# Low parts of weight tiles by accumulating DMAs in place of subtractions

## The chip, the cores and the metric

The kernel runs on one core of a Trainium2 chip. The metric is the device time of one execution in microseconds; the median of three is given. In the profile's names PE is TensorE (matrix products), PEld its weight loads, DVE is VectorE, ACT is ScalarE, POOL is GpSimd and SP is SyncE, which issues most loads.

## The reference

Two layers of an encoder on 512 tokens of 1024 features, in float32:

```python
def rms_norm(x, g):
    y = xf * lax.rsqrt(jnp.mean(xf * xf, axis=-1, keepdims=True) + RMS_EPS)
    return (y * g.astype(F32)).astype(x.dtype)

def swiglu_ffn(x, w_gate, w_up, w_down):          # 1024 -> 2816 -> 1024
    return (jax.nn.silu(x @ w_gate) * (x @ w_up)) @ w_down

for layer in range(DEPTH):                        # DEPTH = 2
    f = swiglu_ffn(rms_norm(h, g[0]), ffn_w_gate[layer, 0], ffn_w_up[layer, 0], ffn_w_down[layer, 0])
    h = h + 0.5 * rms_norm(f, g[1])
    hn = rms_norm(h, g[2])
    # layer 0: m = concat(pool_mixer(z[:512]), s5_mixer(z[512:])) @ ab_w_out, z = hn @ ab_w_in
    # layer 1: m = neighborhood_attention(hn, na_w_qkv, na_rpb, na_w_out)
    h = h + rms_norm(m, g[3])
    f = swiglu_ffn(rms_norm(h, g[4]), ffn_w_gate[layer, 1], ffn_w_up[layer, 1], ffn_w_down[layer, 1])
    h = h + 0.5 * rms_norm(f, g[5])
```

## The kernel before

**Products.** Each float32 operand is split into two 12-bit parts, hi + lo. A product is three passes over parts (`mm3`, L170 to L172): hi x hi, then one low part with the other's hi, then the reverse. In the projections of features on partitions the third pass, L172, takes the weights' low part.

**Weight tiles.** The class `Weights` makes all 128 x 1024 tiles in the order of their use. `_load` has SP load a raw tile from DRAM (`w_raw`, two buffers). `hi` copies it on ScalarE into `w_hi`, which rounds it (L113). `lo` subtracts: `w_lo` = raw - hi (L124), on VectorE, or on GpSimd where a call says so. `fill(n)` emits these splits until n tiles beyond those used up are split; it follows each tile's products (`done`, n = 4), so splits run three to four tiles ahead. `w_hi` and `w_lo` have five buffers.

**Plain tiles and pairs.** In each of the four feed-forwards a part of the gate and up tiles is "plain" (kind p: 24 matmuls of 512 columns). The others are taken as pairs of tiles in Winograd's form: seven products of 12 matmuls of 256 columns, on four derived tiles called g, s, u, h. Tile g is the raw tile itself; s, u and h are sums: `sums` makes them with L95 and L96 on VectorE and L98 on GpSimd. After each pair VectorE adds up the results (L594, L600, L602, and L574 last, when the pair's last product has ended). A gate pair then goes through ScalarE's Silu (L578), the up pair behind it through GpSimd's product with it (L576). `sums` of a pair and its g are emitted after the g product of the pair before it.

**Stages.** Feed-forward (up products, then the down products in two halves), mixer (layer 0: pooling and state space; layer 1: attention), feed-forward, for each layer. Between stages there is a transition: `finish_rows` ends the down products by pairs of token tiles, while the norm of the next stage (`pre_norm`, `to_xT`) runs on ScalarE and VectorE, and `fill(2)`, `fill(4)` split the first tiles of the next stage there, on GpSimd. In the first feed-forward the tables of the state-space mixer are made beside the products by VectorE, ScalarE and DMAs that GpSimd issues. Each engine works through its instructions in the order in which the program emits them.

Of the kernel before, what the change touches and what calls it, by code (L numbers as in the profile page):

```python
# [37 lines left out]
class Weights:  # L38
    """Weight tiles [128, 1024] in the order of their use: loaded, then split into two
    12-bit parts (hi + lo is the float32 value exactly), both ahead of the products.  # L40
    A pair of tiles G = [A11 A12], U = [A21 A22] that is multiplied by Winograd's form of
    Strassen's scheme becomes the tiles g = [A11 A12], s = [S3 -S2], u = [S1 A22], h = [S4]
    with S1 = A21 + A22, S2 = S1 - A11, S3 = A11 - A21, S4 = A12 - S2."""
# [3 lines left out]
    def __init__(self, nc, pool, items, n_split=5):  # L47
# [3 lines left out]
        for item in items:  # L51
            z = {}
# [7 lines left out]
        self.lo_engine = nc.vector  # L60

    def _load(self, tag=None):
# [12 lines left out]
        z[kind] = t  # L75
        self.loaded += 1
# [23 lines left out]
    def source(self, kind, z):  # L100
        """What a tile is split from."""
        if kind in "pg":
            return self._raw("raw", z)
        return {"s": lambda: z["s"], "u": lambda: z["u"][:, HALF:], "h": lambda: z["u"][:, :HALF]}[kind]()

    def hi(self):
        kind, z = self.tiles[self.n_hi]
        src = self.source(kind, z)
        n = src.shape[-1]
        hi, lo = (self.pool.tile([P, 1024], F32R, tag=t, bufs=self.n_split, name=t) for t in ("w_hi", "w_lo"))  # L110
        step = n if kind == "p" else HALF
        for k in range(0, n, step):
            self.nc.scalar.copy(hi[:, k:k + step], src[:, k:k + step])  # L113
        self.hi_lo[self.n_hi] = (hi, lo)
        self.n_hi += 1

    def lo(self, engine=None):
# [6 lines left out]
        (engine or self.lo_engine).tensor_tensor(out=lo[:, :n], in0=src, in1=hi[:, :n].bitcast(F32), op=ALU.subtract)  # L124
# [6 lines left out]
    def fill(self, n, lo_engine=None):  # L131
        """Emits splits until n tiles are split and not used up, loads further."""
# [23 lines left out]
    def done(self, n=1, fill=True):  # L156
        """The products of n more tiles are emitted."""
# [5 lines left out]
class Builder:  # L163
# [14 lines left out]
    def new_psum(self, *halves, **tags):  # L178
        """All eight banks anew: of one kind, or some for each of the tags (number, or number
        and columns), or half for each of two groups of names."""  # L180
# [11 lines left out]
    def rsqrt(self, v):  # L192
        """1 / sqrt(v) of a column pair."""
# [3 lines left out]
    def rsqrt_steps(self, v):  # L197
        """1 / sqrt(v), by steps that return what becomes of it: exponent-halving guess y
        within 3.5%, then y * (1 + d)^(-1/2) for d = v y^2 - 1, by its minimax polynomial on
        that range."""  # L200
# [27 lines left out]
    def chain_begin(self, pool, scale):  # L228
        """What follows a projection m: h += scale * rms_norm(m) * gain, by pairs of token tiles."""
# [5 lines left out]
    def post_pair(self, pair, half, ps):  # L235
        """The vector engine reads one bank while the scalar engine reads the other."""
# [18 lines left out]
    def residual(self, ts, parts=1):  # L255
        """By parts of the columns, each yielded when it is done."""
# [19 lines left out]
    def pre_norm(self, pool, pair, s, gain, order):  # L276
        """Rows of a token pair over their rms; what is returned transposes and splits them."""
# [12 lines left out]
    def to_xT(self, xn, pair, gain, order, between, by_tile=False):  # L290
        """by_tile: the transposes of the first row tile go ahead of all others."""
# [33 lines left out]
    def part(self, x, order, pair):  # L325
        """The columns of a [128, 512] operand that hold the tokens of a pair of token tiles."""
# [10 lines left out]
    def proj_steps(self, ps, w, order, pair=None):  # L337
        """ps[128 output features, tokens] = W[:, 128 columns]^T xT, a step per two k-tiles."""
# [12 lines left out]
    def first_proj(self, n, order, before, start=None, each=None, after=None):  # L351
        """The first n column tiles on the first token pair (the first two by turns), while the
        second pair's norm ends.
        start: what follows that; each: what follows a tile, after: what stands for the
        splits that follow it."""
# [24 lines left out]
    def split_evac(self, hi, lo, src, scale=None, later=None):  # L380
        """hi on the scalar engine, lo on the vector engine; that can be left for later, so
        that the vector engine does not wait for the scalar engine."""
# [18 lines left out]
    def finish_rows(self, cp, psB, tail, kts, lhs, opened, nxt):  # L401
        """The last k-tiles of the second half of the columns, by pairs of token tiles, so that
        the norms of one pair run beside the products of the next."""
# [33 lines left out]
        self.W.fill(2, nc.gpsimd)  # L437
# [4 lines left out]
        self.W.fill(4, nc.gpsimd)  # L442
        return self.pre_norm(cp, 1, finish((2, 3)), nxt[0], nxt[1])

# [1 line left out]
    b_order = list(range(NF))  # L446

    def form_product(self, ps, w, x):
        """ps [128, 256] (+)= a quarter: weights [128, 4 x 128]^T times activations [128, 4, 256]."""
# [7 lines left out]
    def x_sums(self, forms, tmp):  # L457
        """The sums of quarters of xT (B) that Winograd's scheme takes, split, and beside them
        the first tiles of weights, by steps that follow the first column tiles:
        T1 = B12 - B11, T3 = B22 - B12, -T2 = T1 - B22, -T4 = B21 - T2."""  # L460
# [48 lines left out]
    def ffn(self, layer, which, nxt, before, ssm=None):  # L509
        """gate/up with features on partitions, down with tokens on partitions. From feature  # L510
        tile n_plain on, gate and up are taken by pairs of tiles (A1, A2), by halves of the
        contraction and of the tokens, in seven products of a quarter (Winograd).
        nxt: (gain row, order) of the norm that follows, None at the end. ssm: the constants of
        the state-space mixer are made beside it."""
# [5 lines left out]
        def start():  # L520
            """Sums of the activations, beside the last four plain tiles."""
# [94 lines left out]
        # ten slots; the first two lie where memory is free first  # L616
# [74 lines left out]
    # tokens by (column, row): a tile of 128 queries is 16 columns, its keys are 24 or 32 columns  # L691
    KEY0 = (0, 64, 192, 320)
    NKEY = (192, 256, 256, 192)
    # chunks of the keys of a query tile: (offset, number, set of V rows, its first partition)
# [3 lines left out]
    def attention(self, nxt, before):  # L698
# [19 lines left out]
        def evac_q(hp, ps):  # L718
            """By heads: both parts as one contraction, the high one in the rows of the head."""
# [8 lines left out]
        def evac_k(hp, ps):  # L728
            """By heads: the high part twice; the low part of both."""
# [28 lines left out]
        def keys(x, s):  # L758
            """Rows of V: set 0 is the last and the first 64 keys, the others 128 from 64 on."""
# [3 lines left out]
        def v_steps(c):  # L763
            """V of four heads, for all sets: weight tiles of four k-tiles by 256 columns."""
# [20 lines left out]
        self.W.lo_engine = nc.gpsimd  # L785
# [110 lines left out]
        self.W.lo_engine = V  # L896
# [22 lines left out]
    # Chunks of 8 tokens: token 8c + j. Lanes are (a, p) for the group 2 gp + a and the state p;  # L919
    # columns are (direction, gp). U[(h', j)] holds the token j of every chunk.  # L920
    #   m_dram  U -> chunk input of the states, [(h', j), unit, re/im, dir, gp, a, p]
    #   g_dram  C lambda^k, k = 1..8 (8..1 for the backward direction), [(re/-im, p), unit, dir, gp, a, (h, k)]
    #   i_dram  U -> outputs of the same chunk, [(h', j'), g, (j, h)]
# [839 lines left out]
```

## Time and profile before

| | |
|---|---|
| median of three runs | 1957.59 us (1957.04 to 1961.34) |
| span of the profiled execution, first to last instruction (its own time) | 1956.6 us |
| busy, share of the span: PE / PEld / DVE / ACT / POOL | 95% / 84% / 78% / 47% / 22% |
| mean granted TensorE clock | 0.983 |
| DMA moved | 225.47 MB, mean 115 GB/s |
| HBM read / written | 206.69 MB / 18.84 MB |

The span is the profiled execution's time; it lies within 1 us of the median. Busy shares are means over stages with different limits. The clock is a share of full speed: 1 is 2.4 GHz, and the lower level, 0.5, is 1.2 GHz.

### The profile page before, as it was taken

The numbers are of one execution on the slowest core, as the hardware profiler recorded it, in microseconds if no ns is written. First come the engines' busy times: TensorE is split into PE (matmuls) and PEld (weight loads), VectorE is DVE, ScalarE is ACT, GpSimd is POOL, SyncE is SP. The second block draws the span as 40 slices with busy tenths as digits, with TensorE's granted clock in tenths as the row PEclk, the third lists the DMA queues.
The fourth block names the chain that finished last, engine by engine and source line by source line (L and its number), as shares of the span: only waits on it lengthen the run. The fifth ranks groups of instructions, "written<-read, shape, count | busy, mean of one in ns | idle before, by whom it ended". The sixth has DMA issues, their size and how long they took to land.

```text
span 1956.6 us, 31540 instructions
## 1 busy us (share of the span) xinstructions
PE 1864.5 (95%) x12368; PEld 1652.2 (84%) x12368; DVE 1519.5 (78%) x2357; ACT 916.9 (47%) x1725; POOL 423.9 (22%) x267
## 2 busy tenths in 40 slices
PE   7999999998889999999899999999999989999998
PEld 7877987886678999888799997879878788999886
DVE  6788979968679999844899996465565589999744
ACT  5244455455454444533544445346555455444432
POOL 1024221014014223100432330011222023322100
PEclk9999999999999999999999999999999999999999
DMA  5464246537422233322223323223222222332321
GB/s 189 136 204 158 104 142 199 186 114 254 150 87 98 101 105 109 108 97 75 76 97 109 108 87 119 97 76 108 98 97 98 73 79 92 103 108 98 119 90 62
DMA packets 82020, 225.47 MB, mean 115 GB/s; under 512 B 15792, under 2 KB 20048, under 8 KB 80848
## 3 DMA queue, kind: packets, MB, share of 16 engines
q1 hardware_dynamic: 70176, 197.80, 29.3%
q0 software_dynamic: 6960, 23.57, 4.0%
q10 hardware_dynamic: 4736, 2.10, 0.4%
q8 instruction: 97, 1.59, 0.3%
q14 instruction: 51, 0.42, 0.1%
HBM read 206.69 MB, written 18.84 MB: 115 GB/s over the span
## 4 chain that ended last, share of the span: by engine, by line
PE 43%; DVE 16%; issue 9%; ACT 5%; DMA 1%; POOL 0%; DVEq 0%; ACTq 0%; POOLq 0%
PE ps_gu L172 4%; PE ps_gu L170 4%; PE ps_gu L171 4%; PE ps_A L172 3%; PE ps_A L170 3%; PE ps_A L171 3%; PE ps_B L172 3%; PE ps_B L171 3%; PE ps_B L170 3%; PE ps_f L170 3%; DVE w_s L96 3%; DVE w_lo L124 2%; PE ps_f L172 2%; PE ps_f L171 2%; ACT w_hi L113 1%
## 5 line engine op out<-in xcount | busy, mean ns | idle before, releaser
L124 DVE TENSOR_TENSOR w_lo<-w_raw,w_hi 128x1024 fp32r<-128x1024 f32 x209 | 275.8, 1325 | 218.4 <-ACT w_hi L113 218.4
L113 ACT CAST w_hi<-w_raw 128x1024 fp32r<-128x1024 f32 (+1 forms) x313 | 261.7, 863 | 270.9 <-PE ps_A L172 83.5
L172 PE MATMUL ps_gu<-xsum,w_lo 128*128 128x256 f32 x1088 | 309.5, 284 | 9.7 <-DVE w_lo L124 9.7
L172 PE MATMUL ps_gu<-xT_hi,w_lo 128*128 128x256 f32 (+1 forms) x1008 | 311.7, 309 | 1.3 <-DVE w_lo L124 1.0
L171 PE MATMUL ps_gu<-xsum,w_hi 128*128 128x256 f32 x1088 | 306.8, 282 | 3.4 <-DVE xsum L470 3.2
L170 PE MATMUL ps_gu<-xsum,w_hi 128*128 128x256 f32 x1088 | 308.0, 283 | 0.0
L170 PE MATMUL ps_gu<-xT_hi,w_hi 128*128 128x256 f32 (+1 forms) x1008 | 307.8, 305 | 0.0
L171 PE MATMUL ps_gu<-xT_lo,w_hi 128*128 128x256 f32 (+1 forms) x1008 | 306.8, 304 | 0.0
L172 PEld LDWEIGHTS ps_gu<-xsum,w_lo 128*128 128x128 f32 x1088 | 207.4, 191 | 11.4 <-DVE w_lo L124 11.4
L171 PEld LDWEIGHTS ps_gu<-xsum,w_hi 128*128 128x128 f32 x1088 | 208.0, 191 | 4.9 <-DVE xsum L470 4.9
L124 POOL TENSOR_TENSOR w_lo<-w_raw,w_hi 128x1024 fp32r<-128x1024 f32 x36 | 86.0, 2393 | 582.0 <-DVE rs_q L215 377.3
L170 PEld LDWEIGHTS ps_gu<-xsum,w_hi 128*128 128x128 f32 x1088 | 208.1, 191 | 0.0
L172 PEld LDWEIGHTS ps_gu<-xT_hi,w_lo 128*128 128x128 f32 x1008 | 191.9, 190 | 17.0 <-DVE w_lo L124 7.6
L170 PEld LDWEIGHTS ps_gu<-xT_hi,w_hi 128*128 128x128 f32 x1008 | 191.9, 190 | 10.0 <-issue 1.1
L171 PEld LDWEIGHTS ps_gu<-xT_lo,w_hi 128*128 128x128 f32 x1008 | 192.2, 191 | 8.7
L98 POOL TENSOR_TENSOR w_u<-w_raw,w_s 128x512 f32<-128x512 f32 x68 | 121.2, 1782 | 277.5 <-ACT w_hi L113 168.1
L113 ACT CAST w_hi<-w_s 128x512 fp32r<-128x512 f32 x136 | 77.5, 619 | 200.0 <-DVE w_s L96 193.5
L172 PE MATMUL ps_A<-w_hi,gT 128*128 128x512 f32 x352 | 141.2, 401 | 12.2 <-DVE gT L630 12.2
L576 POOL TENSOR_TENSOR g<-g,m 128x1024 f32<-128x1024 f32 x34 | 93.0, 2734 | 258.4 <-DVE m L574 258.4
L96 DVE TENSOR_TENSOR w_s<-w_raw,w_u 128x1024 f32<-128x1024 f32 x68 | 145.8, 2143 | 2.4
L170 PE MATMUL ps_A<-w_hi,gT 128*128 128x512 f32 x352 | 140.9, 400 | 0.0
L171 PE MATMUL ps_A<-w_lo,gT 128*128 128x512 f32 x352 | 140.3, 398 | 0.0
(375 smaller groups left out, 4376.7 us busy)
## 6 DMA issues: line engine op xcount, KB each, us to landing
w_raw<-in_w_gu_dram SPq DMA_DIRECT2D x106, 512.0 KB, 3.3
w_raw<-in_w_dn_dram SPq DMA_DIRECT2D x88, 512.0 KB, 3.2
w_u<-in_w_gu_dram SPq DMA_DIRECT2D x70, 512.0 KB, 3.6
w_raw<-in_w_qk_dram SPq DMA_DIRECT2D x16, 512.0 KB, 3.2
bias<-in_att_bias_dram SPq DMA_DIRECT2D x16, 512.0 KB, 4.1
w_raw<-in_w_in_dram SPq DMA_DIRECT2D x8, 512.0 KB, 3.2
cm<-m_dram SPq DMA_DIRECT2D x4, 1024.0 KB, 8.7
w_raw<-in_w_ao_dram SPq DMA_DIRECT2D x8, 512.0 KB, 4.0
```

The costliest lines, as they stand in the source:

```text
L96: tt(out=blocks(s), in0=g[:, :HALF].unsqueeze(1).broadcast_to([P, 2, HALF]), in1=blocks(u)[:, :2], op=ALU.subtract)
L98: self.nc.gpsimd.tensor_tensor(out=u[:, :HALF], in0=g[:, HALF:], in1=s[:, HALF:], op=ALU.add)
L113: self.nc.scalar.copy(hi[:, k:k + step], src[:, k:k + step])
L124: (engine or self.lo_engine).tensor_tensor(out=lo[:, :n], in0=src, in1=hi[:, :n].bitcast(F32), op=ALU.subtract)
L170: mm(ps, a[0], b[0], start=start, stop=False)
L171: mm(ps, a[0], b[1], start=False, stop=False)
L172: mm(ps, a[1], b[0], start=False, stop=stop)
L576: nc.gpsimd.tensor_tensor(out=rows(f), in0=rows(f), in1=m, op=ALU.mult)
```

## The change

The low part of a tile that comes straight from DRAM (kinds p and g) is no longer subtracted by an engine. ScalarE writes the negative of the rounded tile into `w_lo` right behind the copy into `w_hi`, and GpSimd issues a DMA that reads the tile from DRAM once more and adds it onto `w_lo`. The low parts of s, u and h are subtracted by VectorE as before (one of them by GpSimd at each start of the pairs). The choices of GpSimd as the engine for `lo` elsewhere fall away.

```diff
 def _load(self, tag=None):
...
         z[kind] = t
+        z[kind + "_src"] = src
         self.loaded += 1
...
 def hi(self):
...
         for k in range(0, n, step):
             self.nc.scalar.copy(hi[:, k:k + step], src[:, k:k + step])
+        if kind in "pg":
+            self.nc.scalar.mul(lo, src, -1.0)
         self.hi_lo[self.n_hi] = (hi, lo)
...
 def lo(self, engine=None):
...
         if kind == "g":
             self.sums(z)
         hi, lo = self.hi_lo[self.split]
-        (engine or self.lo_engine).tensor_tensor(out=lo[:, :n], in0=src, in1=hi[:, :n].bitcast(F32), op=ALU.subtract)
+        if kind in "pg":
+            self.nc.gpsimd.dma_start(lo, z["raw_src"], accum_op=ALU.add)
+        else:
+            (engine or self.nc.vector).tensor_tensor(out=lo[:, :n], in0=src, in1=hi[:, :n].bitcast(F32),
+                                                     op=ALU.subtract)
...
 def finish_rows(self, cp, psB, tail, kts, lhs, opened, nxt):
...
-        self.W.fill(2, nc.gpsimd)
+        self.W.fill(2)
...
-        self.W.fill(4, nc.gpsimd)
+        self.W.fill(4)
...
 def attention(self, nxt, before):
...
-        self.W.lo_engine = nc.gpsimd
...
-        self.W.lo_engine = V
...
 def first_norm(self, gain, order):
...
-        self.W.lo(nc.gpsimd)
+        self.W.lo()
...
-        self.W.fill(4, nc.gpsimd)
+        self.W.fill(4)
```

Line numbers of the changed kernel differ: L95, L96, L98 are L98, L99, L101 there, L124 is L132, L574 and L576 are L583 and L585, L594, L600 and L602 are L603, L609 and L611; the negative is L118 and the accumulating DMA L130.

GpSimd's queue at the start of the second feed-forward's pairs and for the pairs next behind it (L485 and L486 make a sum of the activations `xT_hi` and `xT_lo`; the name `g` is the buffer that these and the feed-forward's product L576 are kept in); before:

```order
L98 TENSOR_TENSOR w_u<-w_raw,w_s 128x512
L485 TENSOR_TENSOR g<-g,xT_hi 128x1024
L486 TENSOR_TENSOR g<-g,xT_lo 128x1024
L124 TENSOR_TENSOR w_lo<-w_u,w_hi 128x512
L98 TENSOR_TENSOR w_u<-w_raw,w_s 128x512 x2
L576 TENSOR_TENSOR g<-g,m 128x1024
L98 TENSOR_TENSOR w_u<-w_raw,w_s 128x512 x2
L576 TENSOR_TENSOR g<-g,m 128x1024
```

And of the changed kernel, at the same place:

```order
L101 TENSOR_TENSOR w_u<-w_raw,w_s 128x512
L130 DMA w_lo<-in_w_gu_dram 128x1024
L494 TENSOR_TENSOR g<-g,xT_hi 128x1024
L495 TENSOR_TENSOR g<-g,xT_lo 128x1024
L132 TENSOR_TENSOR w_lo<-w_u,w_hi 128x512
L101 TENSOR_TENSOR w_u<-w_raw,w_s 128x512
L130 DMA w_lo<-in_w_gu_dram 128x1024
L101 TENSOR_TENSOR w_u<-w_raw,w_s 128x512
L130 DMA w_lo<-in_w_gu_dram 128x1024
L585 TENSOR_TENSOR g<-g,m 128x1024
L101 TENSOR_TENSOR w_u<-w_raw,w_s 128x512
L130 DMA w_lo<-in_w_gu_dram 128x1024
```

Each pair's g has a DMA behind the sum L101, and that sum behind the product L585 where there is one; before, none of g's work stood in this queue.

VectorE's queue for one steady pair, from L574 to the next L574; before:

```order
L574 TENSOR_TENSOR m<-m,ps_gu 128x512
L95 TENSOR_TENSOR w_u<-w_u 128x512
L96 TENSOR_TENSOR w_s<-w_raw,w_u 128x1024
L124 TENSOR_TENSOR w_lo<-w_raw,w_hi 128x1024
L594 TENSOR_TENSOR m<-m,ps_gu 128x2x256
L124 TENSOR_TENSOR w_lo<-w_s,w_hi 128x1024
L600 TENSOR_TENSOR m<-m,ps_gu 128x512
L602 TENSOR_TENSOR m<-m,ps_gu 128x256
L124 TENSOR_TENSOR w_lo<-w_u,w_hi 128x1024
L124 TENSOR_TENSOR w_lo<-w_u,w_hi 128x512
```

And of the changed kernel:

```order
L583 TENSOR_TENSOR m<-m,ps_gu 128x512
L98 TENSOR_TENSOR w_u<-w_u 128x512
L99 TENSOR_TENSOR w_s<-w_raw,w_u 128x1024
L603 TENSOR_TENSOR m<-m,ps_gu 128x2x256
L132 TENSOR_TENSOR w_lo<-w_s,w_hi 128x1024
L609 TENSOR_TENSOR m<-m,ps_gu 128x512
L611 TENSOR_TENSOR m<-m,ps_gu 128x256
L132 TENSOR_TENSOR w_lo<-w_u,w_hi 128x1024
L132 TENSOR_TENSOR w_lo<-w_u,w_hi 128x512
```

The subtraction for g, directly behind the sums, has gone; the rest keeps its order.

ScalarE's queue at the transition from the second feed-forward of layer 0 to the first of layer 1 (`xn` and `xT_hi` are the norm of the next stage, `junk` its sums of squares); before:

```order
L226 ACTIVATE junk,ss_8992<-ps_B 128x512
L113 CAST w_hi<-w_raw 128x1024
L286 ACTIVATE xn<-h,rs_r 128x512 x2
L318 ACTIVATE xT_hi<-ps_t,gcol 128x256 x4
L226 ACTIVATE junk,ss_8992<-ps_B 128x512
L318 ACTIVATE xT_hi<-ps_t,gcol 128x256 x4
L113 CAST w_hi<-w_raw 128x1024 x2
L226 ACTIVATE junk,ss_h<-h 128x1024 x2
L286 ACTIVATE xn<-h,rs_r 128x512 x2
```

And of the changed kernel:

```order
L116 CAST w_hi<-w_raw 128x1024
L118 ACTIVATE w_lo<-w_raw 128x1024
L295 ACTIVATE xn<-h,rs_r 128x512 x2
L327 ACTIVATE xT_hi<-ps_t,gcol 128x256 x4
L235 ACTIVATE junk,ss_9116<-ps_B 128x512
L327 ACTIVATE xT_hi<-ps_t,gcol 128x256 x4
L116 CAST w_hi<-w_raw 128x1024
L118 ACTIVATE w_lo<-w_raw 128x1024
L116 CAST w_hi<-w_raw 128x1024
L118 ACTIVATE w_lo<-w_raw 128x1024
L235 ACTIVATE junk,ss_h<-h 128x1024 x2
L295 ACTIVATE xn<-h,rs_r 128x512 x2
```

A negative stands behind each copy of a raw tile, once ahead of the first token pair's `xn`, twice ahead of the second pair's sums of squares.

## Rows read from the trace of the kernel before

**Rows 1.** Windows: PE, PEld, DVE, ACT, POOL busy us, clock, DMA share, GB/s.

```profile
300.00:350.00 50.00, 46.70 (x230) 35.94 (x229) 49.00 (x108) 30.16 (x67) 10.09 (x16) 0.97 0.64 207
...
450.00:500.00 50.00, 35.44 (x470) 29.88 (x469) 49.33 (x53) 23.30 (x33) 21.40 (x22) 0.90 0.71 245
...
700.00:750.00 50.00, 50.00 (x419) 49.64 (x419) 47.78 (x51) 23.34 (x44) 13.66 (x7) 1.00 0.32 109
...
850.00:900.00 50.00, 50.00 (x216) 40.27 (x215) 21.85 (x27) 18.81 (x27) 0.00 (x0) 1.00 0.27 93
```

**Rows 2.** Timeline of TensorE in the pairs: start, us, instruction.

```profile
700.77 0.28 PE L170 MATMUL ps_gu<-xsum,w_hi 128*128 128x256 f32 x1
...
706.43 0.28 PE L170 MATMUL ps_gu<-xT_hi,w_hi 128*128 128x256 f32 x1
...
720.97 0.28 PE L170 MATMUL ps_gu<-xsum,w_hi 128*128 128x256 f32 x1
```

**Rows 3.** Timeline of VectorE behind an up pair.

```profile
712.42 0.68 DVE L574 TENSOR_TENSOR m<-m,ps_gu 128x512 f32<-128x512 f32 x1
...
713.74 3.30 DVE L96 TENSOR_TENSOR w_s<-w_raw,w_u 128x1024 f32<-128x1024 f32 x1
```

**Rows 4.** Timeline of GpSimd in the same pairs.

```profile
705.61 1.30 POOL L98 TENSOR_TENSOR w_u<-w_raw,w_s 128x512 f32<-128x512 f32 x1 [6.47 <-ACT w_hi L113]
...
713.25 2.72 POOL L576 TENSOR_TENSOR g<-g,m 128x1024 f32<-128x1024 f32 x1 [6.34 <-DVE m L574]
...
717.18 2.16 POOL L98 TENSOR_TENSOR w_u<-w_raw,w_s 128x512 f32<-128x512 f32 x1 [1.21 <-DVE w_s L96]
```

**Rows 5.** Page, groups: count, busy us, mean ns, idle time before.

```profile
L124 DVE TENSOR_TENSOR w_lo<-w_raw,w_hi 128x1024 fp32r<-128x1024 f32 x209 | 275.8, 1325 | 218.4 <-ACT w_hi L113 218.4
...
L124 POOL TENSOR_TENSOR w_lo<-w_raw,w_hi 128x1024 fp32r<-128x1024 f32 x36 | 86.0, 2393 | 582.0 <-DVE rs_q L215 377.3
...
L96 DVE TENSOR_TENSOR w_s<-w_raw,w_u 128x1024 f32<-128x1024 f32 x68 | 145.8, 2143 | 2.4
```

**Rows 6.** Timelines of ScalarE and TensorE at the start.

```profile
12.69 1.05 ACT L113 CAST w_hi<-w_raw 128x1024 fp32r<-128x1024 f32 x1 [0.38 <-DMA w_raw<-in_w_gu_dram]
...
14.16 0.58 PE L170 MATMUL ps_p<-xT_hi,w_hi 128*128 128x256 f32 x1 [0.66 <-ACT xT_hi L318]
```

**Rows 7.** DMA view: a queue's load, and issues with median us to landing.

```profile
q1 hardware_dynamic: 70176, 197.80, 29.3%
...
w_raw<-in_w_dn_dram SPq DMA_DIRECT2D x88, 512.0 KB, 3.2
...
w_raw<-in_w_ao_dram SPq DMA_DIRECT2D x8, 512.0 KB, 4.0
...
free<-in_ssm_bt_dram POOLq DMA_DIRECT2D x3, 512.0 KB, 5.2
...
free<-in_ssm_c_dram POOLq DMA_DIRECT2D x1, 512.0 KB, 3.8
...
free<-kept_lp POOLq DMA_DIRECT2D x1, 288.0 KB, 8.3
```

**Rows 8.** Timelines of TensorE and GpSimd at a start of the pairs.

```profile
984.24 0.29 PE L170 MATMUL ps_gu<-xT_hi,w_hi 128*128 128x256 f32 x1
...
984.46 2.22 POOL L98 TENSOR_TENSOR w_u<-w_raw,w_s 128x512 f32<-128x512 f32 x1 [5.29 <-DVE w_s L96]
```

**Rows 9.** Timelines of ScalarE, VectorE, TensorE at a transition.

```profile
940.15 1.98 ACT L113 CAST w_hi<-w_raw 128x1024 fp32r<-128x1024 f32 x2
...
941.27 2.40 DVE L209 TENSOR_TENSOR rs_u<-rs_u,rs_y 128x2 f32<-128x2 f32 x1
...
953.30 2.62 PE L297 MATMUL ps_t<-ident,xn 128*128 128x128 f32 x16 [3.81 <-ACT xn L286]
```

**Rows 10.** Timeline of TensorE in down products, with its waits.

```profile
328.93 0.50 PE L172 MATMUL ps_A<-w_hi,gT 128*128 128x512 f32 x1 [2.13 <-DVE gT L630]
...
811.67 0.50 PE L172 MATMUL ps_A<-w_hi,gT 128*128 128x512 f32 x1 [2.18 <-DVE gT L630]
```

More of the change, by code (lines that the diff above doesn't have):

```diff
@@ L59, in __init__ @@
         self.live = {k: 0 for k in self.BUFS}
-        self.lo_engine = nc.vector
     def _load(self, tag=None):
```

## The prediction

> **What bounds the kernel now.** I read the busy times by 50 us windows first, because the stages have different limits. In the down products (850:900) TensorE is busy for the whole window and VectorE for 21.85 of 50 us; in the feature pairs (700:750) TensorE shows 50.00 and VectorE 47.78; in the state-space part of the first layer (300:350, 450:500) VectorE is at 49.00 and 49.33 of 50 and TensorE has holes [rows 1]. So the kernel is TensorE bound nearly everywhere, with VectorE as its equal in the pairs and above it in the state-space part. What the change can win is what TensorE loses there to VectorE; what it can lose is any place where the new low part comes later than the subtraction did.
>
> How much TensorE loses in the pairs is read from its timeline. Between 700.77 and 706.43 us there are 48 matmuls without a hole, 0.1179 us each. A pair has 84 (7 products of 12), two pairs 168, so TensorE needs 19.81 us. From 700.77 to 720.97, two pairs later, it takes 20.20 [rows 2]. It loses 0.39 us per two pairs; there are 68 pairs (the count of L96 [rows 5]), so at most 13 us can be won in them.
>
> Next the order of events in a pair on VectorE and GpSimd. Behind an up pair, L574 starts at 712.42 as soon as the last product's sums are in and VectorE gets there, the sums for the next pair but one run beside GpSimd's L576 of 2.72 us, L96 takes 3.30 and ends at 717.04 (over both kinds of pair its mean is 2.14, so behind a gate pair about 1.0). GpSimd's L98 starts at 717.18 [rows 3 to 5]. VectorE's subtraction for tile g stands right behind L96: today the low part of g does not wait for L98.
>
> **What the change removes.** 209 subtractions on VectorE (275.8 us) and 36 on GpSimd (86.0 us) [rows 5]. It adds 245 copies with a factor -1 on ScalarE, 1.05 us each by the copy of the same shape [rows 6], 257 us on an engine that is busy for 47% of the span; and 245 accumulating transfers of 512 KB, issued by GpSimd.
>
> **The unknown: from issue to landing, L.** No accumulating transfer is in the trace. The floor is a plain GpSimd load of the same size, 3.8 us; the ceiling is the longest GpSimd load, 8.3 us (a smaller one, in a crowd) [rows 7]. An accumulation must also fetch the old contents: 512 KB once more through the 16 engines. The main queue moved 197.80 MB in 29.3% of the span, which is 1.52 us for 512 KB [rows 7]. That gives 5.3. L98's end, which releases the accumulation, also frees the raw tile and so starts the next raw load, and the two meet; a raw load in the crowded mixer takes 4.0 instead of 3.2 us, and I take half of that, 0.4 [rows 7]. I use L = 5.7, which is nearer the floor, because the pairs' windows move only 109 GB/s.
>
> The Trainium skill, "DMA: Bandwidth & Descriptors", section "Anatomy of one DMA", fits a GpSimd load as 2.0 us plus bytes over 436 GB/s: 3.2 us here, where the row has 3.8. By that page, with the second fetch at the same rate, L would be 4.4 and the whole sum about zero; the row decides, so the sum goes by 5.7.
>
> **Steady pairs.** VectorE is relieved of 1.33 us a pair [rows 5], so it no longer runs late and L574 starts when the products end. From there the new chain behind an up pair is: 4.76 us to the start of L98 (712.42 to 717.18), 1.30 us for L98 (as at 705.61; I put the 2.16 at 717.18 down to the subtraction beside it, which is gone), then L [rows 3, 4]: 6.06 + L. The pair that TensorE does meanwhile takes 9.90. TensorE's third matmul of the next pair needs the low part, so the stall is L - 3.84 = 1.86 us. The gate pair behind has no L576 ahead of its sums and is 2 us shorter, and uses the time of the stall: no stall of its own. Two pairs take 19.81 + 1.86 = 21.67 instead of 20.20: +1.47. Counting 30 of the 34 up pairs (the first of each of the four layers stands below): **+44 us**. With L at 3.8 it is -12, at 8.3 +122.
>
> **Starts of the pairs**, four times. VectorE is late there with the sums of the activations. The second pair's L98 ends at 986.68, with one subtraction fewer ahead at 985.5; plus 5.7 is 991.2. TensorE begins the last product of the first pair at 984.24, is through with it after 12 matmuls at 985.66 and needs the low part at 985.9 [rows 8]. 5.3 us late, four times: **+21 us** (14 to 32).
>
> **Transitions**, five times (after the end of a mixer or feed-forward). Two opposite changes. ScalarE's two copies at 940.15 become four; the third tile's low part is issued at 942.1, when copy and negative are done, and lands at 947.8, and TensorE has 46 matmuls of the third and fourth tile behind it, to 953.3. Against that GpSimd no longer makes two subtractions of 2.39 us [rows 5], beside which VectorE's L209 took 2.40 us for two columns, so the second token pair's chain is over 4 us earlier; its transposes began at 953.30 after a hole of 3.81 us [rows 9]. They begin at the same time: **0** (-9 to +13 for all five).
>
> **Start of the kernel.** The second tile's high part is made from 12.69 to 13.74; with two negatives its own is written at 15.3 and the low part lands at 21.0. The first products run at 14.16 now [rows 6], and at 15.9 when ScalarE is later by two copies: **+5 us** (3 to 8).
>
> **Plain tiles, 177.** 24 matmuls a tile, 216 in 50 us: 5.56 us a tile [rows 1]. The split runs three to four tiles ahead, 16.7 us at least; copy, negative, issue and landing are 8.4. Nothing, hidden by the tiles ahead; if L rose past 14 each tile would cost the rest. But in 300:350 the transfer engines are 64% busy already, and 9 accumulations of 2 x 1.52 us add 55%. What is over 100% of 50 us would be 9.5 us; the first 150 us are alike. Bounds 0 and 27; I take **+6 us**, because three tiles of lead swallow most.
>
> **What comes back.** At the four changes from pairs to down products TensorE waits for VectorE (2.18 us at 811.67, alike in the others): -9. In the state-space part the wait at 328.93 (2.13) and a lesser one go, and with them the slow clock behind: the granted clock is 0.97 over 50 us, 1.5 us: -5 [rows 1, 10]. In 450:500 four subtractions leave a full VectorE: -4. Together **-18 us**.
>
> Sum: 44 + 21 + 5 + 6 - 18 = +58 on the profiled span of 1956.6, which lies 1 us below the median of 1957.59: **2015 us**. The forecast is slower, by 3%.
>
> **Rivals.** *The relief wins* (the other sign): the accumulations land like plain loads, L = 4.0. Then the pairs win 7, starts cost 15, the kernel's start 3, transitions win 8, and 18 comes back: -15, 1943 us; at 3.8, 1936. For it: the floor row, and that fetch from SBUF and fetch from DRAM may overlap. Against: the same 16 engines do both. It decides below L = 4.4, where the sum is zero. Chance 0.23.
> *Accumulations are slow*: L about 8.3, or more by a narrower adder. 122 + 32 + 8 + 13 + 6 - 18 = +163, 2121 us, and more if stalls of 4 us bring the slow clock, as the holes in 300:350 and 450:500 did (0.97 and 0.90) [rows 1]. For it: crowded GpSimd loads. Chance 0.21. The Trainium skill, "SBUF — State Buffer", section "Who interferes with whom", says that GpSimd cannot write descriptors while VectorE runs an operation in its two-port mode; by that L would grow where VectorE is full. Here VectorE's work is two-input arithmetic, and the GpSimd loads issued at a full VectorE (300:350) landed in 5.2 us [rows 7], so the trace shows no such block.
> *The transfers become the bound* in the first layer only, at the upper 27 us in place of 6: 2036 us, chance 0.06. For it the 64%, against it the lead.
> *Nothing measurable*: L near 4.4, 1958 us, chance 0.04.
> The forecast, L from 4.9 to 6.8, 1981 to 2064 us by the same terms: 0.46.
>
> **Range.** 1938 to 2115 takes in the forecast, the zero, most of the relief and the nearer part of the slow case. The forecast's own range is 1981 to 2064. A measurement of this kernel can tell 0.2% (4 us) from no change. Faster 0.23 (the relief), within 0.2% 0.04, slower 0.73 (the other three).
>
> **What would show it.** The transfers table gives L for the low parts directly: 5 to 6.5 right, below 4.4 the relief, above 8 the slow case. In the pairs, TensorE's or its weight loads' waits for the low part should appear behind up pairs only, 1.9 us each, and VectorE fall from 47.8 to about 42 of 50 us. The hole of 2.18 at the change to the down products should be gone; the transitions should keep a hole of about 4 us, now before the third tile. In 300:350 the holes should go and the transfer share rise above 0.9. The prediction is wrong if the pairs' two-pair period stays at 20.2 or less, or if VectorE stays late there so that the chain begins later than I take it.

## The result, and the profile after

The changed kernel takes 2204.36 us (median of four runs, 2200.9 to 2215.34), the one before 1958.26: a ratio of 1.1266, interval 1.1236 to 1.1296. The sign was the one forecast, the size four times it: 246 us in place of 57, and above the range. The profiled execution took 2200.9 us, its span is 2199.1.

Where the 242.5 us of the two spans lie, by stages: from the first matmul of a stage to that of the next in TensorE's timeline, summed over stages of one kind. The transition into the mixer of layer 0 is counted with the mixer.

| stages | before | after | lost | forecast |
|---|---|---|---|---|
| start, plain gate and up tiles | 189.4 | 207.4 | +18.0 | +11 |
| pairs (four stages, 68 pairs) | 711.8 | 859.7 | +147.9 | +65 |
| down products (four) | 520.7 | 537.9 | +17.1 | -14 |
| mixer and attention | 400.7 | 448.5 | +47.8 | -4 |
| transitions (the other four) | 134.0 | 145.7 | +11.7 | 0 |

The page of the changed kernel, busy times, and the two large DMA queues (packets, MB, share of 16 engines); before, the hardware queue stood at 29.3% [rows 7].

```profile
PE 1928.0 (88%) x12368; PEld 1703.4 (77%) x12368; DVE 1216.0 (55%) x2147; ACT 1157.9 (53%) x1972; POOL 516.4 (23%) x477
...
q0 software_dynamic: 42528, 153.08, 36.0%
q1 hardware_dynamic: 70176, 197.80, 28.7%
```

VectorE is relieved as announced (55% for 78%), and nothing comes of it. TensorE has 88% for 95%. Next its waits (engine, line, for what: us in total, times, longest):

```profile
PE ps_gu L181 <- DMA w_lo<-in_w_gu_dram: 137.1, 69, 8.6
...
PE ps_p L181 <- DMA w_lo<-in_w_gu_dram: 27.1, 9, 5.4
...
PE ps_A L180 <- DMA w_lo<-in_w_dn_dram: 15.8, 6, 3.6
```

Of the 69 waits, some 2 us each, 64 are in the 68 pairs, the others at plain tiles of the first layer: nearly every pair waits for its low part, not every second one. The DMA view says how long a transfer takes (KB each, median us from issue to landing):

```profile
w_lo<-in_w_gu_dram POOLq DMA_DIRECT2D x108, 512.0 KB, 7.6
w_raw<-in_w_gu_dram SPq DMA_DIRECT2D x106, 512.0 KB, 4.0
w_raw<-in_w_dn_dram SPq DMA_DIRECT2D x88, 512.0 KB, 6.5
w_lo<-in_w_dn_dram POOLq DMA_DIRECT2D x88, 512.0 KB, 7.9
```

L is 7.6 to 7.9, where 5.7 was taken, and the raw loads are later as well (3.2 before for the down tiles [rows 7]). The first row takes in plain gate and up tiles; for the pairs alone, the four stages have medians of 6.9 to 7.3. Windows of 50 us with the columns of [rows 1]: plain tiles of the first layer, mixer, a start of the pairs, steady pairs, down products.

```profile
150.00:200.00 50.00, 44.86 (x221) 34.07 (x221) 27.79 (x55) 26.38 (x57) 21.64 (x26) 0.97 0.99 273
...
550.00:600.00 50.00, 35.81 (x300) 28.38 (x301) 24.24 (x31) 21.68 (x27) 4.38 (x5) 0.86 0.61 173
...
1100.00:1150.00 50.00, 36.42 (x269) 35.81 (x267) 41.20 (x39) 24.69 (x40) 20.04 (x12) 0.83 0.49 115
...
1850.00:1900.00 50.00, 43.83 (x361) 42.81 (x359) 36.70 (x42) 23.43 (x39) 14.52 (x11) 1.00 0.57 136
...
1400.00:1450.00 50.00, 50.00 (x216) 40.27 (x215) 11.65 (x18) 27.09 (x36) 7.75 (x9) 1.00 0.90 191
```

Steady pairs: 361 matmuls in 50 us where 419 stood [rows 1]. Down products: still full at a transfer share of 0.90. The mean granted clock fell from 0.983 to 0.947, so 233 us of the span were at 1.2 GHz instead of 67 (twice what is missing to 1, times the span).

The timeline of two steady pairs and of one start of the pairs shows who is late (start, us, instruction, idle time before and its releaser):

```profile
1875.84 0.69 DVE L583 TENSOR_TENSOR m<-m,ps_gu 128x512 f32<-128x512 f32 x1
...
1877.09 0.39 PE L181 MATMUL ps_gu<-xT_hi,w_lo 128*128 128x256 f32 x1 [1.06 <-DMA w_lo<-in_w_gu_dram]
...
1880.60 1.29 POOL L101 TENSOR_TENSOR w_u<-w_raw,w_s 128x512 f32<-128x512 f32 x1 [1.21 <-DVE w_s L99]
1881.84 0.86 POOL L130 DMA_DIRECT2D w_lo<-in_w_gu_dram  x1
...
1881.92 0.33 SPq L76 DMA_DIRECT2D w_raw<-in_w_gu_dram  x1
...
1888.74 0.39 PE L181 MATMUL ps_gu<-xT_hi,w_lo 128*128 128x256 f32 x1 [1.42 <-DMA w_lo<-in_w_gu_dram]
...
1890.24 0.37 ACT L596 COPY m<-ps_gu 128x256 f32<-128x256 f32 x1 [1.28 <-PE ps_gu L181]
1890.51 1.14 ACT L116 CAST w_hi<-w_raw 128x512 fp32r<-128x512 f32 x2
1891.55 1.06 ACT L118 ACTIVATE w_lo<-w_raw 128x1024 fp32r<-128x1024 f32 x1
...
1892.67 0.33 SPq L76 DMA_DIRECT2D w_raw<-in_w_gu_dram  x1
...
1892.91 0.87 POOL L130 DMA_DIRECT2D w_lo<-in_w_gu_dram  x1 [1.80 <-ACT w_lo L118]
...
1900.27 0.39 PE L181 MATMUL ps_gu<-xT_hi,w_lo 128*128 128x256 f32 x1 [1.30 <-DMA w_lo<-in_w_gu_dram]
...
1103.36 0.86 POOL L130 DMA_DIRECT2D w_lo<-in_w_gu_dram  x1
...
1110.20 0.58 PE L181 MATMUL ps_gu<-xT_hi,w_lo 128*128 128x256 f32 x1 [8.28 <-DMA w_lo<-in_w_gu_dram]
```

Three things. Behind the up pair the chain is as forecast: 1875.84 to the issue at 1881.84, 6.0 us (6.06 was said), then the landing. Behind the gate pair there is a second chain that the prediction did not have: TensorE's wait ends at 1888.74, ScalarE's L596 waits for that product, the copy and the negative stand behind L596, and GpSimd issues at 1892.91: a loop of 4.2 us plus the landing per pair. And the load of the next raw tile is issued within 0.3 us of each accumulating transfer (1881.92, 1892.67), because both are released when the engines are through with the old raw tile. Two pairs take 23.18 us (1877.09 to 1900.27) for 20.20 [rows 2]. That is a stretch at full clock; from the third pair of a stage on, two pairs took 23.4 to 24.6 us on average, at a mean granted clock of 0.956 to 0.982.

### The profile page after: what moved, and what is told of

It reads as the page before. It is cut to its first block, busy times and chain, and to the rows that moved or that the text cites. A ratio compares the mean times of both kernels' runs of the same rounds, so it can differ in the third digit from the quotient of the medians.

```text
span 2199.1 us, 32028 instructions
## 1 busy us (share of the span) xinstructions
PE 1928.0 (88%) x12368; PEld 1703.4 (77%) x12368; DVE 1216.0 (55%) x2147; ACT 1157.9 (53%) x1972; POOL 516.4 (23%) x477
## 3 DMA queue, kind: packets, MB, share of 16 engines
HBM read 336.19 MB, written 18.84 MB: 161 GB/s over the span
## 4 chain that ended last, share of the span: by engine, by line
PE 28%; issue 20%; DMA 17%; DVE 6%; POOL 3%; ACT 3%; POOLq 0%; DVEq 0%; ACTq 0%
DMA w_lo<-in_w_gu_dram 15%; PE ps_gu L181 4%; PE ps_gu L179 3%; PE ps_gu L180 3%; PE ps_A L180 3%; PE ps_A L181 3%; PE ps_A L179 3%; PE ps_B L180 3%; PE ps_B L179 3%; PE ps_B L181 3%; POOL w_lo L130 1%; DVE w_s L99 1%; DMA w_lo<-in_w_dn_dram 1%; DVE w_lo L132 1%; ACT w_lo L118 1%
## 5 line engine op out<-in xcount | busy, mean ns | idle before, releaser
L181 PE MATMUL ps_gu<-xT_hi,w_lo 128*128 128x256 f32 (+1 forms) x1008 | 332.8, 330 | 137.2 <-DMA w_lo<-in_w_gu_dram 137.1
L181 PEld LDWEIGHTS ps_gu<-xT_hi,w_lo 128*128 128x128 f32 x1008 | 210.3, 209 | 161.6 <-DMA w_lo<-in_w_gu_dram 152.7
L639 DVE TENSOR_TENSOR gT<-g,gT 128x512 fp32r<-128x512 f32 x176 | 120.4, 726 | 260.7 <-ACT gT L638 260.6
L118 ACT ACTIVATE w_lo<-w_raw 128x1024 fp32r<-128x1024 f32 x245 | 258.9, 1057 | 0.0
L116 ACT CAST w_hi<-w_u 128x512 fp32r<-128x512 f32 (+1 forms) x206 | 121.6, 623 | 158.7 <-PE ps_gu L181 105.5
L181 PE MATMUL ps_p<-xT_hi,w_lo 128*128 128x256 f32 (+1 forms) x416 | 129.4, 311 | 39.8 <-DMA w_lo<-in_w_gu_dram 27.1
L101 POOL TENSOR_TENSOR w_u<-w_raw,w_s 128x512 f32<-128x512 f32 x68 | 91.0, 1338 | 291.2 <-DVE w_s L99 142.9
L603 DVE TENSOR_TENSOR m<-m,ps_gu 128x512 f32<-128x512 f32 x68 | 46.7, 687 | 202.1 <-PE ps_gu L181 185.8
L130 POOL DMA_DIRECT2D w_lo<-in_w_dn_dram x88 | 76.2, 865 | 345.3 <-ACT w_lo L118 303.2
L130 POOL DMA_DIRECT2D w_lo<-in_w_gu_dram x108 | 94.9, 897 | 245.3 <-ACT w_lo L118 244.2
```

Source lines behind the costliest of these rows:

```text
L101: self.nc.gpsimd.tensor_tensor(out=u[:, :HALF], in0=g[:, HALF:], in1=s[:, HALF:], op=ALU.add)
L118: self.nc.scalar.mul(lo, src, -1.0)
L130: self.nc.gpsimd.dma_start(lo, z["raw_src"], accum_op=ALU.add)
L181: mm(ps, a[1], b[0], start=False, stop=stop)
L603: V.tensor_tensor(out=quarters(m)[:, 0:4:3], in0=quarters(m)[:, 1:2].broadcast_to([P, 2, 256]), in1=quarters(m26), op=ALU.add)
L639: V.tensor_tensor(out=lo, in0=graw[:, f], in1=hi.bitcast(F32), op=ALU.subtract)
```

## Experiments

Two theories of the 7.6 us: the transfer is that slow by itself, or it is slowed by the raw load that starts with it. Rivals of both: ScalarE's work, and the traffic. Line numbers differ a little from kernel to kernel.

**Plain loads in place of accumulating ones.**

```diff
-            self.nc.gpsimd.dma_start(lo, z["raw_src"], accum_op=ALU.add)
+            self.nc.gpsimd.dma_start(lo, z["raw_src"])
```

> The 245 transfers no longer add, they only write the raw tile into the low part (so the low parts hold the whole tile and the products are not the reference's); waits, queue and ScalarE's negatives stay. Theory (the price is the adding transfer's own time from issue to landing, 7.6 us, twice a plain load): it lands in about 4 us, the loop of a pair through ScalarE (4.2 us plus the landing) is under 9.9 and the chain behind an up pair stalls by 0.4 at most, so 1960 to 1990 us. Rival 1 (the added DRAM traffic and GpSimd's queue are the price): the traffic is the same, 2100 us or more. Rival 2 (ScalarE's 259 us of negatives are the price): unchanged, about 2200.

The low parts hold the whole tile here; the kernel leaves out the addition. 2030.88 us (2027.34 to 2034.42), 1.037 of before. The transfers land in:

```profile
w_lo<-in_w_gu_dram POOLq DMA_DIRECT2D x108, 512.0 KB, 5.0
...
w_lo<-in_w_dn_dram POOLq DMA_DIRECT2D x88, 512.0 KB, 4.7
```

173 us of the 246 go with the adding, at the same traffic (336.19 MB read from HBM in both). But a plain load takes 5.0 here, not the 3.8 of [rows 7]. In the pairs the stall is now behind up pairs alone (9.97 and 11.05 us in turn, 21.0 for two): the prediction's formula, 19.81 + L - 3.84, gives 20.97. The time came out 40 us above what was expected: the landing was taken as about 4 us, and ScalarE's work as nothing. No run parts the two; the next one has ScalarE's work alone.

**Negatives without transfers**: the kernel before, `self.nc.scalar.mul(lo, src, -1.0)` added in `hi` for tiles from DRAM.

> The kernel before, with ScalarE's negatives added ahead of the subtractions, which overwrite them; no transfer is added and the result is the reference's. Theory: 1.06 us each on an engine with slack, and a subtraction that waits for it: 1960 to 1975 us. Rival 2 (ScalarE's negatives are the price): above 2050.

1993.20 us (1990.49 to 1994.02), ratio 1.0177 (1.0160 to 1.0194): 35 us. Two steady pairs take 20.50 for 20.20. Neither theory's number: ScalarE's work is no main cause, but it is not free.

**One kind of tile alone** (the condition `kind in "pg"` cut to one kind; the others subtracted as before).

> Only the 177 plain tiles are made by negatives and adding transfers; the 68 tiles g of the pairs are subtracted as before. Theory: the pairs return to 20.2 us per two, what stays is the 94 us lost outside the pair stages: about 2050 us. Rival 1 (traffic): the loss goes by the number of transfers, 177 of 245, about 2133.

2087.64 us (2087.32 to 2087.95).

> Only the 68 tiles g are made by adding transfers; plain tiles as before. Theory: the pair stages keep their loss of 148 us and the rest returns: about 2105 us, two pairs taking some 23 us. Rival 1 (traffic): 68 of 245 of the loss, about 2026.

2103.51 us (2101.47 to 2105.55). The second is as the theory has it; the first loses 130 us in place of 94. The parts add to 275, more than the whole. Most of what is over lies in the pair stages: e4's lose 160 us where the changed kernel's lose 148, and e3's, with every tile g subtracted, lose 11. Why is not shown. A loss by number of transfers is ruled out: 68 transfers cost more than 177.

**Transfer ahead of the sums.**

```diff
-        if kind == "g":
-            self.sums(z)
         hi, lo = self.hi_lo[self.split]
         if kind in "pg":
             self.nc.gpsimd.dma_start(lo, z["raw_src"], accum_op=ALU.add)
-        else:
+        if kind == "g":
+            self.sums(z)
+        if kind not in "pg":
```

> The changed kernel, with the transfer of a tile g issued ahead of the pair's sums, so that it no longer stands behind L101 in GpSimd's queue. Theory A (the loop of a pair goes through ScalarE: the copy of the first product's sums waits for TensorE, the negative stands behind it, 4.2 us plus the landing of 7.3 make 11.5 a pair): only the up pairs gain, by 0.5 us; two pairs still take 22.9, 2185 to 2204 us. Theory B (the chain of the prediction, sums and L101 ahead of the transfer, is what binds): the stall behind up pairs goes, two pairs take about 21.5, 2150 us or less.

2089.49 us (2086.03 to 2092.95): 115 us back by order alone. Two steady pairs take 20.3, and theory A fails as I put it: ScalarE's loop is still there and binds little. The reason is in the timeline of GpSimd and SP, and in the DMA view:

```profile
1888.63 0.87 POOL L128 DMA_DIRECT2D w_lo<-in_w_gu_dram  x1 [8.19 <-ACT w_lo L118]
1889.24 1.59 POOL L101 TENSOR_TENSOR w_u<-w_raw,w_s 128x512 f32<-128x512 f32 x1
...
1890.86 0.33 SPq L76 DMA_DIRECT2D w_raw<-in_w_gu_dram  x1
```

```profile
w_lo<-in_w_gu_dram POOLq DMA_DIRECT2D x108, 512.0 KB, 5.4
```

The raw load now starts 2.2 us behind the transfer (L101, which frees the raw tile, comes after it), and the transfer lands in 5.4 instead of 7.6. The order moved two things at once, so it had to be taken apart (below).

**ScalarE's copy behind the split too.** L596 is moved behind `self.W.done()`.

> As the last, and ScalarE's copy of the first product's sums (L596) is put behind the split of the next pair's g, so that the rounded tile and the negative no longer wait for TensorE. Theory A: the loop through ScalarE is cut and the issue comes 1.5 us earlier or more; two pairs take 20.3 to 21.5, the pair stages fall by 90 to 140 us in all, 2070 to 2120 us. Theory B: like the run before, since ScalarE was not what bound.

2078.69 us (2077.86 to 2079.52). All steady pairs now take 9.97. The loop through ScalarE was worth 11 us once the landing was short, not the 90 or more that were expected.

**Two halves**: each transfer as two of 512 columns.

> The changed kernel, with each adding transfer issued as two of 256 KB. If the 7.6 us go with the bytes, a half lands in 4 to 5 us, and TensorE, which needs the first half first in the pairs, waits less: 2120 to 2190 us. If they are mostly a fixed cost of an adding transfer, a half takes 6 us or more, the second issue costs GpSimd 0.9 us more: 2200 to 2280.

2131.20 us (2123.56 to 2138.83). In the pairs the first half mostly lands 5.6 to 6.4 us after its issue, the whole tile of the changed kernel in 6.9 to 7.3: half the bytes save about a microsecond, but TensorE takes the first half first. The time is that of the first guess, the landing nearly that of the second.

**Only the pairs' tiles, with both orders.**

> Adding transfers for the tiles g alone, transfer ahead of the sums and ScalarE's copy behind the split; plain tiles as in the kernel before. Theory A: the pairs as in e6, the rest as before less 2.2 us at each of three changes to the down products: 1955 to 2000 us. Theory B: near 2100, as e4.

1957.18 us (1953.52 to 1959.92), ratio 0.9999 (0.9988 to 1.0009). Two steady pairs 19.95, the holes at the changes to the down products gone, but one hole at the third pair of each stage:

```profile
618.76 1.06 ACT L584 ACTIVATE g<-m 128x1024 f32<-128x1024 f32 x1 [3.61 <-DVE m L580]
619.72 1.12 ACT L114 CAST w_hi<-w_raw 128x512 fp32r<-128x512 f32 x2
620.75 1.06 ACT L116 ACTIVATE w_lo<-w_raw 128x1024 fp32r<-128x1024 f32 x1
...
622.35 0.87 POOL L126 DMA_DIRECT2D w_lo<-in_w_gu_dram  x1 [8.62 <-ACT m L595]
...
627.54 0.39 PE L178 MATMUL ps_gu<-xT_hi,w_lo 128*128 128x256 f32 x1 [2.43 <-DMA w_lo<-in_w_gu_dram]
```

**The raw load alone moved.** The changed kernel in its own order; VectorE reads one column of the raw tile when it gets to u, and only then is the tile free.

```diff
+        if kind == "u":
+            self.nc.vector.tensor_copy(out=self.hold, in_=z["raw"][:, :1])
-        if kind in "pg":
+        if kind in "pu":
             self._free(z, "raw")
```

> The changed kernel in its own order (sums, L101, transfer), but the raw tile of a pair is held until VectorE gets to the pair's u (one column of it is read there), so that the load of the next raw tile starts about 4 us after the adding transfer and not in the same 0.3 us. Theory C (what made 5.3 us into 7.3 in the pairs is the raw load that the same event starts): the transfers land in 5.2 to 5.5 us there, the loop through ScalarE is under 9.9, only the stall behind up pairs stays (6.05 + 5.3 - 9.9 = 1.5 us), two pairs take 21.4: 2090 to 2140 us. Rival D (it is the place in GpSimd's queue, ahead of the sums, that won in e5; the landing time fell as a by-product): 7 us or more and about 2200, or later, since raw tiles come later.

2112.67 us (2112.52 to 2112.82): theory C, and 92 us by one start time (and one short read on VectorE). Its timeline, and its DMA view:

```profile
1856.33 0.87 POOL L131 DMA_DIRECT2D w_lo<-in_w_gu_dram  x1
...
1860.00 0.34 SPq L77 DMA_DIRECT2D w_raw<-in_w_gu_dram  x1
...
1840.17 0.39 PE L184 MATMUL ps_gu<-xT_hi,w_lo 128*128 128x256 f32 x1 [1.70 <-DMA w_lo<-in_w_gu_dram]
...
1861.53 0.39 PE L184 MATMUL ps_gu<-xT_hi,w_lo 128*128 128x256 f32 x1 [0.94 <-DMA w_lo<-in_w_gu_dram]
```

```profile
w_lo<-in_w_gu_dram POOLq DMA_DIRECT2D x108, 512.0 KB, 5.3
```

Only every second pair waits, behind up pairs (10.08 and 11.25 in turn); two take 21.36. This is the picture that the prediction drew.

**The same for plain tiles.** The kernel with the transfer ahead, and GpSimd reads one column of a plain raw tile behind the issue.

> e5 (transfer ahead of the sums), and for the plain tiles GpSimd reads one column of the raw tile behind the issue, so that the next raw load starts about 1 to 2 us after the adding transfer. Theory C: the plain tiles' transfers fall from 7.9 to 5.5 to 6.8 us and the stages where they are late (start, first layer, mixers, transitions) get some of it back: 2040 to 2075 us. Rival D: 7.9 and 2089 us, or later by the new instruction.

2091.27 us (2089.00 to 2093.55): the landings did what theory C says, the time did not.

```profile
w_lo<-in_w_dn_dram POOLq DMA_DIRECT2D x88, 512.0 KB, 6.8
w_lo<-in_w_qk_dram POOLq DMA_DIRECT2D x16, 512.0 KB, 5.2
```

By stages the mixer of layer 0 wins 10 us and the last three down products 12. The first layer's down products give 12 back and the pairs 5. In the former the second half takes 84 us where it took 66, since there the raw load is what is late:

```profile
419.70 1.04 ACT L117 CAST w_hi<-w_raw 128x1024 fp32r<-128x1024 f32 x1 [14.87 <-DMA w_raw<-in_w_dn_dram]
```

**Transfers from the fourth pair of a stage on**, and a control with ScalarE's copy alone moved in the kernel before.

> e8, but in each of the four stages of pairs the first three tiles g are subtracted as before and only those from the fourth on are made by adding transfers, because e8 still showed one hole of 2.4 to 4.1 us for the low part at the third pair of each stage. Theory: these holes and the slow clock behind them go; steady pairs stay at 19.95 per two and the changes to the down products without a hole: 1938 to 1952 us. Rival: the first three pairs lose to VectorE what the hole cost: 1955 to 1960.

1960.76 us (1956.65 to 1964.69), ratio 1.0017 (1.0007 to 1.0027): missed. The hole of about 3 us went along to the first pair with a transfer.

> A control: the kernel before with nothing but ScalarE's copy of the first product's sums put behind the split, as in e6, e8 and e11. If what e11 wins is the transfers', this is 1955 to 1960 us; if it is the order on ScalarE, it wins as much as e11.

1956.79 us (1952.51 to 1959.44), ratio 0.9993 (0.9984 to 1.0003).

**Silu behind the split too.** In e8 the copy and the negative stood behind the Silu, which waited for VectorE (3.61 us above).

```diff
-                nc.scalar.activation(out=rows(f), in_=m, func=AF.Silu)
+                silu.append((rows(f), m))
...
+                while silu:
+                    g, x = silu.pop()
+                    nc.scalar.activation(out=g, in_=x, func=AF.Silu)
```

The second part stands behind L596's copy, itself behind `self.W.done()`.

> e8 (adding transfers for the tiles g alone, transfer ahead of the sums, ScalarE's copy behind the split), and ScalarE's Silu of a gate pair is put behind the next split too. In e8 and e11 the first transfers of a stage were late because the rounded tile and the negative stood behind the Silu, which waits for L574's successor on a late VectorE. Theory: the issue comes 1.5 us earlier, the holes of 2.4 to 4.1 us shrink or go with the slow clock behind them: 1935 to 1950 us. Rival (the next wait in line, VectorE's late sums or the raw tile, takes their place): 1953 to 1960.

1936.95 us (1933.88 to 1938.39), ratio 0.9895 (0.9878 to 0.9912).

> The control: both orders on ScalarE (copy and Silu behind the split) in the kernel before, with subtractions and no transfer. If what e14 wins is the transfers', this is 1953 to 1960 us; if it is the order, it wins as much.

1937.49 us (1936.46 to 1938.02), ratio 0.9900 (0.9884 to 0.9916): as fast, without one accumulating transfer. Windows of steady pairs, with the transfers first:

```profile
1000.00:1050.00 50.00, 50.00 (x424) 50.00 (x423) 41.22 (x46) 27.71 (x48) 18.89 (x13) 1.00 0.59 156
```

And with the orders alone:

```profile
1000.00:1050.00 50.00, 50.00 (x424) 50.00 (x423) 49.66 (x51) 24.13 (x44) 19.57 (x9) 1.00 0.32 110
```

In both TensorE is busy throughout and two pairs take 19.95 us, close to the floor of 19.81 in the prediction; VectorE is at 41.22 in one and at 49.66 in the other.

**Only the down products' tiles.**

> Adding transfers for the 88 tiles of the down products alone, everything else subtracted as before. Theory (a transfer is hidden where the split runs three tiles ahead, 16.7 us, and shows in full where it does not, at a stage's first tiles and in the mixers): the last three down products lose only at their first tile, the first layer's, where the transfers' share is high, loses 5 to 12 us: 1962 to 1985 us. Rival (the plain tiles' loss goes by their number): 88 of 177 of what e3 lost, 130 us, which is 65: about 2022.

1993.82 us (1992.88 to 1997.21), ratio 1.0187 (1.0170 to 1.0204), 9 us above the theory's range and far under the rival's. In the last three feed-forwards TensorE waits once for a low part, 6.1 to 6.9 us at the first tile, and not at the other 21 of each; the first layer's down products lose 15 us.

## Why the prediction was right in sign and wrong in size

**The landing time, L: the first step that failed.** "I use L = 5.7" was 3.8 + 1.52 for the second fetch + 0.4 for sharing. The first two terms hold together: with the raw load started 2 us or more behind, the transfers of the pairs land in 5.1 to 5.3 (medians by stage, e5 and e9), where the two make 5.3. The third was mis-sized: 0.4 is 1.6 to 2.0 in the pairs (6.9 to 7.3) and 2.6 in the down products (7.9). The prediction had seen that L98's end starts both, and priced it by how late raw loads come in a crowded stage. In the pairs the raw load is hardly held up (3.2 to 3.9 us) and the transfer bears it; in the down products both do (6.5 and 7.9). In e5 it is the load that bears it, started 2.2 us behind: 4.6 us in the pairs. e9 moved the load's start, and 92 us came back. Which part of the way the two share is not shown.

The trace of the kernel before had a hint. GpSimd issues these two loads mostly 0.54 us apart, and their medians are 5.6 and 6.8 us, not the 3.8 of the floor:

```profile
ssm_tab<-in_ssm_bt_dram POOLq DMA_DIRECT2D x5, 512.0 KB, 5.6
ssm_tab<-l_dram POOLq DMA_DIRECT2D x5, 512.0 KB, 6.8
```

Nor was 8.3 the longest GpSimd load: the rows are medians, and one load of 512 KB, issued at 281.50 in a row of others, took 10.9.

L alone does not give the size. By the prediction's own terms an L of 8.3, above the medians measured, makes +163 us, and 246 were measured. Its terms for the pairs make 154 of it, near the 148 measured; those outside the pairs make 9, where 95 were lost (plain tiles, below).

The Trainium skill, "Collectives: The Full Stack", section "The bandwidth ceiling", says of a collective, reduce-scatter, that its add needs two source reads and that it therefore runs at about half the rate of a gather. The trace of this DMA agrees: from the software queue's shares, with and without adding (36.0% of 2199.1 us and 22.0% of 2025.6, less 4.0% of 1956.6 for its other work), 245 transfers hold the 16 engines for 2.9 and 1.5 us each.

**Steady pairs.** The formula was right at three landing times: 20.97 for 21.0 at 5.0, 21.07 for 21.36 at 5.1, 23.0 for 23.18 at 7.0. "No stall of its own" for the gate pair was wrong for the changed kernel: the loop through ScalarE closes at 4.2 + L > 9.9, that is from L = 5.7 on. At 7 us the stall was shared between both kinds of pair; the sum was still the formula's. Of the 148 us of the pair stages, 34 times 2.9 us, about 99, are this.

**Starts of the pairs.** Forecast at 5.3 each, behind the second pair's L98. The first pair's low part, taken as safe, is the later one: 8.28 us at 1110.20, since its transfer waits for sums on a VectorE busy with the activations; two of the pairs behind it waited 3.6 and 2.9 us more there. The rest of the 148 us I put down to these and the clock; no run parts them.

**Plain tiles: the second step that failed.** "The split runs three to four tiles ahead" holds inside the last three down products, and there the transfers are hidden as said (e16; 0.90 transfer share and a full TensorE). It does not hold at a stage's first tile, in the mixers and at the transitions, which the sum did not price or put at zero: the mixer and the attention alone lost 47.8 us, the longest of their waits 7.95 us for `w_glu`. Outside the pair stages 95 us were lost where -7 was forecast. With e1's plain loads (4.7 us for the down tiles) it is 14: the landing shows there too. In the first layer the transfer share reached 0.99 as feared, and 6 us were too few: 18 with the kernel's start, and 11 in its down products.

**ScalarE.** 257 us of negatives were priced at nothing in the steady state. They measured 258.9 in the profile and cost 35 us when alone (e2). How much of that is in the whole, behind longer waits, is not shown.

**What comes back.** -18 did not come: at the changes to the down products the wait for VectorE became one for the first low part (3.24 us at 940.57). Where only the pairs' tiles are transferred it does go (e8).

**The clock.** As a cost it was in the slow rival alone. By TensorE's timeline, matmuls at about twice their usual distance cost 34 us before and 85 after: some 50 of the 242 us. The windows above with a low clock (0.83 and 0.86) are ones with long holes; no run separates the two.

**What bounds.** The prediction took VectorE, at 47.78 of 50 us, as TensorE's equal in the pairs, and what TensorE lost there, "at most 13 us", as lost to VectorE. e15 keeps all of VectorE's work and wins 19 us: by the stages of the two profiles 6 in the pairs and 12 in the down products, where the waits of 2.18 us for VectorE go (and 4 at the start, ahead of what was moved). So VectorE was late there because of ScalarE's order: copy and Silu, which wait for TensorE and VectorE, stood ahead of the rounding that VectorE waits for. The copy moved alone wins nothing (e13); the Silu alone was not tried. e14, which relieves VectorE as well, wins no more than e15: with the order put right, the relief of the likeliest rival has nothing left to win in the pairs.

## What to carry to other kernels

A transfer that takes the place of an instruction is priced by its landing beside what the same event starts, not by itself: look at which load is freed by the instruction that issues it, and give the transfer a head start. Two engines near 100% in a window do not show which bounds: first look at what stands ahead of whom in the in-order queue of a third engine with slack. And a control that makes the new version's order changes without its idea can show that the idea won nothing.

## What the runs showed of the hardware

An accumulating transfer of 512 KB from DRAM into SBUF landed in 5.1 to 5.4 us with the next load issued 2 us or more behind it (pairs of e5, e9), and in 7 to 8 us beside a raw load of 512 KB issued within 0.3 us. That load itself came in 3.9 us in the pairs and 6.5 in the down products (3.2 without the transfers). Half the size landed mostly in 5.6 to 6.4 beside such a load (e7). GpSimd was busy 0.87 us for a typical adding issue, 0.53 to 0.59 for a plain one (e1).
